# Where the moving operand starts: rows of x shifted by 40 bytes in a one-layer hybrid decoder kernel

## The chip, the cores and the metric

The kernel runs on one core of one Trainium2 chip. The metric is the device time of one execution in microseconds; three runs of the kernel before gave 1689.64, 1690.13 and 1691.94, with the median 1690.13. One further execution was taken with the hardware profiler; all rows of the profile come from that one.

## The reference

One inference step of a decoder layer with three groups of heads, on 256 prompt rows and 8 single-row samples, so 264 rows of 4096 numbers, all in float32. The layer normalises h, projects it with one large matrix, runs three mixers on slices of the projection, gates them, and projects back:

```python
hn = rmsnorm(h, norm_gain)
P = einsum('btd,de->bte', hn, w_in)          # 4096 -> 13324 columns
A = sink_attention(...) * silu(z_a)          # sliding window, 12 heads
B = mlstm_chunkwise(...) * sigmoid(o) * silu(z_m)
C = u * (tril(W_s) @ layernorm(gelu(v)) + b) * silu(z_c)
h = h + concat(A, B, C) @ w_out              # 4096 -> 4096
y = rmsnorm(h, final_gain)
```

Beside y it returns the window's rows of keys and values, the states of B and the normalised rows of C. The two projections hold nearly all of the arithmetic.

## The kernel before, in words

All activations are kept transposed: a row of x in this text is one k-tile of 128 channels, on the 128 partitions, with the 264 positions along the free dimension. There are 32 such rows (KT).

**The projections.** float32 operands are split into a high and a low part of the type float32r, which TensorE streams in one pass. x becomes `xh` and `xl`, a weight tile becomes `wh` and `wl`, and a product is made of three matmuls: wh with xh, wh with xl, wl with xh. The weights are the stationary operand (128 by 128) and a row of xh or xl is the moving one (128 by 264). The output columns are handled in groups of 512: 26 groups for the first matrix and 8 for the second. Each group runs over 16 chunks of two k-tiles; a chunk has four column tiles with two k-tiles each and three matmuls for each, 24 in all, which accumulate into four PSUM tiles named `mp`. That makes 34 x 16 x 24 = 13056 main matmuls.

**The supply of weights.** `load_w` fetches a chunk (512 KB) into one of three `wf` buffers through SyncE's DMA queue, four chunks ahead. `split_w`, two chunks ahead, has ScalarE copy it to `wh` (rounded to the high part) and VectorE subtract to get `wl`. Both have three buffers.

**The rows of x.** `split_x` (lines 244 to 253) writes xh and xl during the first group from `yb`, which holds x; `split_y` (lines 292 to 294) writes them again ahead of the second matrix from the mixers' results, which by then stand in `yb`. Nothing else writes these two tiles, and nothing but the main matmuls and the subtraction that makes xl reads them.

**The order of the work.** Instructions are emitted in one order, written out by hand: ahead of each column tile the small generators of the mixers get a turn (`tick`), when a simple running estimate of each engine's time says that they will not hold up the rest. The estimate goes by the kind of an instruction and the sizes of its operands. So small matmuls of the mixers and transposes stand between main matmuls, on the same engine.

**Places in SBUF.** Bytes are counted within a partition. `xh` starts at 1280 and `xl` at 42240, each with 32 rows of ROW = 320 numbers, 1280 bytes, of which the first 264 numbers are used. Both starts and the row length are multiples of 256. The tile `pad0` ahead of them (PAD0, 32 numbers) makes it so. `yb` follows at 83200 with rows of 264 numbers, 1056 bytes, without padding. A second unused tile, `pad1` (PAD1, 24 numbers), stands ahead of `acc`; the weights come behind that, with `wh` at 136448, 140544 and 144640 and `wl` at 148736, 152832 and 156928. These too are multiples of 256, and a stationary operand starts at a multiple of 512 bytes within its buffer.

The matmuls at the heart of it:

```python
PE.matmul(out, wh[:, kk, s], xh[:, k], start=(k == 0), stop=False)
PE.matmul(out, wh[:, kk, s], xl[:, k], start=False, stop=False)
PE.matmul(out, wl[:, kk, s], xh[:, k], start=False, stop=(k == KT - 1))
```

Line 205 of the profile is the helper through which all engines' calls go, so that groups are told apart by the names of their tiles.

Of the kernel before, what the change touches and what calls it, by code (L numbers as in the profile page):

```python
# [11 lines left out]
F32R = mybir.dt.float32r  # L12
# [6 lines left out]
P = 128  # L19
D = 4096  # L20
KT = D // P
TP = 256
TS = 8
T = TP + TS
# [45 lines left out]
LAG = 6.0  # L70
NCH = KT // KK
ROW = 320
PAD0, PAD1 = 32, 24

SM = {}
# [15 lines left out]
def body(tc, xt, wi, wg, wo, sm, kc, vc, c0, wst, w00, bs, cgain, cbias,  # L91
# [3 lines left out]
    with ExitStack() as ctx:  # L95
        cp = ctx.enter_context(tc.tile_pool(name="const", bufs=1))
# [28 lines left out]
        keep = Phase("keep")  # L125

        cp.tile([P, PAD0], F32, name="pad0")
        xh = cp.tile([P, KT, ROW], F32R, name="xh")[:, :, :T]
        xl = cp.tile([P, KT, ROW], F32R, name="xl")[:, :, :T]
        yb = cp.tile([P, KT, T], F32, name="yb")  # L130
        sms = cp.tile([P, NSM], F32, name="sms")
        ones = cp.tile([P, P], F32, name="ones")
# [1047 lines left out]
```

## Time and profile before

| | |
|---|---|
| median of three runs | 1690.13 us |
| the profiled execution | 1690.53 us |
| its span, first to last instruction | 1687.7 us |
| TensorE busy | 1663.3 us, 13754 matmuls |
| VectorE busy | 911.6 us |
| ScalarE busy | 739.1 us |
| DMA, mean | 195 GB/s |
| mean granted TensorE clock | 0.995 |

Times in a profile are microseconds unless marked ns. PE is TensorE's matmuls, PEld its weight loads, DVE VectorE, ACT ScalarE, POOL GpSimd, SPq SyncE's queue. A row of a group has the output and the inputs by their names in the program, the shapes, the count, the busy time with the mean of one instruction, and then the idle time of the engine just ahead of these instructions with what ended it. In a list of one tile's instructions the three numbers are the shortest, the median and the longest in ns. In a table of windows a row has the stretch, its length, the busy time with the count of records that overlap the stretch, the granted clock, the DMA engines' mean share and GB/s. In a timeline a row has the start in us from the start of the span, the duration, the engine and the instruction; in the chain of waits, the start, the time and the count. Matmuls are pipelined: a record of one lasts longer than the time to the next one's start.

### The profile page before, as it was taken

The numbers are of one execution on the slowest core, as the hardware profiler recorded it, in microseconds if no ns is written. First come the engines' busy times: TensorE is split into PE (matmuls) and PEld (weight loads), VectorE is DVE, ScalarE is ACT, GpSimd is POOL, SyncE is SP. The second block draws the span as 40 slices with busy tenths as digits, with TensorE's granted clock in tenths as the row PEclk, the third lists the DMA queues.
The fourth block names the chain that finished last, engine by engine and source line by source line (L and its number), as shares of the span: only waits on it lengthen the run. The fifth ranks groups of instructions, "written<-read, shape, count | busy, mean of one in ns | idle before, by whom it ended". The sixth has DMA issues, their size and how long they took to land.

```text
span 1687.7 us, 32534 instructions
## 1 busy us (share of the span) xinstructions
PE 1663.3 (99%) x13754; PEld 1646.4 (98%) x13754; DVE 911.6 (54%) x1277; ACT 739.1 (44%) x971; POOL 80.9 (5%) x82
## 2 busy tenths in 40 slices
PE   9999999999999999999999999999999999999995
PEld 9999999999999999999999999999999999999995
DVE  6565644555544455556665666444666554444445
ACT  6554433444434343444444444334454444344442
POOL 0000000000000000001001100000100030000002
PEclk9999999999999999999999999999999999999998
DMA  8555568545455555667767666555656656555553
GB/s 297 172 181 178 184 191 278 157 156 165 151 173 178 184 179 184 205 205 234 229 215 241 216 226 214 185 179 185 204 176 224 203 192 192 187 180 184 180 182 147
DMA packets 102177, 328.91 MB, mean 195 GB/s; under 512 B 11090, under 2 KB 24328, under 8 KB 102032
## 3 DMA queue, kind: packets, MB, share of 16 engines
q1 hardware_dynamic: 101072, 326.04, 60.4%
q8 instruction: 107, 1.75, 0.4%
q10 hardware_dynamic: 960, 0.81, 0.1%
q14 instruction: 38, 0.31, 0.0%
HBM read 314.20 MB, written 12.60 MB: 194 GB/s over the span
## 4 chain that ended last, share of the span: by engine, by line
PE 96%; DVE 2%; DMA 1%; ACT 1%; issue 0%; SPq 0%; DVEq 0%; ACTq 0%
PE mp L205 92%; PE mx L205 3%; DVE wl L205 1%; DVE yb L205 1%; DMA wf<-wo 1%; PE sn L205 0%; ACT wh L205 0%; DMA wf<-wi 0%; PE gps L205 0%; DVE rstd L205 0%; DVE TM L205 0%; ACT es L205 0%; DVE mvs L205 0%; ACT L205 0%; ACT yb L205 0%
## 5 line engine op out<-in xcount | busy, mean ns | idle before, releaser
L205 PE MATMUL mp<-xh,wh 128*128 128x264 f32 x4352 | 1242.5, 286 | 2.5 <-ACT wh L205 1.9
L205 PE MATMUL mp<-xh,wl 128*128 128x264 f32 x4352 | 1231.3, 283 | 2.6 <-DVE wl L205 2.5
L205 PE MATMUL mp<-xl,wh 128*128 128x264 f32 x4352 | 1230.9, 283 | 0.0
L205 DVE TENSOR_TENSOR wl<-wf,wh 128x1024 fp32r<-128x1024 f32 (+1 forms) x545 | 685.3, 1261 | 741.1 <-ACT wh L205 734.5
L205 ACT ACTIVATE wh<-wf 128x1024 fp32r<-128x1024 f32 (+1 forms) x545 | 574.9, 1057 | 808.6 <-PE mp L205 712.1
L205 PEld LDWEIGHTS mp<-xh,wh 128*128 128x128 f32 x4352 | 819.0, 188 | 9.3 <-issue 5.6
L205 PEld LDWEIGHTS mp<-xh,wl 128*128 128x128 f32 x4352 | 819.0, 188 | 3.9 <-DVE wl L205 3.9
L205 PEld LDWEIGHTS mp<-xl,wh 128*128 128x128 f32 x4352 | 819.2, 188 | 0.4
L205 POOL TENSOR_TENSOR acc<-acc,es 128x264 f32<-128x264 f32 x29 | 21.9, 756 | 412.4 <-ACT es L205 410.3
L205 ACT ACT_TABLE_LOAD x22 | 28.2, 1283 | 1.2 <-PEq L1160 0.8
L205 POOL TENSOR_SCALAR_AFFINE_SELECT tmp<-bc 128x128 f32<-128x128 f32 x12 | 5.1, 448 | 491.8 <-DMA bc<-gd 446.0
L205 ACT ACTIVATE es<-yb 128x264 f32<-128x264 f32 x37 | 15.2, 412 | 17.7 <-DVE yb L205 17.7
L205 POOL TENSOR_TENSOR cb<-cb,bc 128x2056 f32<-128x2056 f32 x6 | 22.5, 3748 | 0.2 <-PE mx L205 0.2
L205 ACT ACTIVATE bias<-bias,ar 128x128 f32<-128x128 f32 (+1 forms) x24 | 10.7, 448 | 24.9 <-DVE ar L205 24.8
L205 POOL MEMSET pad<- 128x1024 f32 x2 | 1.9, 950 | 409.5 <-PE mx L205 409.5
L205 ACT ACTIVATE es<-et 128x264 f32<-128x264 f32 x32 | 12.6, 419 | 17.1 <-DVE yb L205 13.8
L205 DVE SCALAR_TENSOR_TENSOR cb<-vb,wsk,cb 128x257 f32<-128x257 f32 x48 | 20.1, 481 | 0.0
L205 ACT ACTIVATE xh<-yb 128x264 fp32r<-128x264 f32 x32 | 12.1, 412 | 17.7 <-DVE yb L205 17.7
L205 DVE TENSOR_TENSOR et<-mp,rstd 128x264 f32<-128x264 f32 x52 | 18.8, 424 | 0.0
L205 ACT ACTIVATE yb<-yb,sms 128x264 f32<-128x264 f32 x32 | 16.5, 517 | 1.0
L205 DVE TENSOR_TENSOR yb<-yb,rstd 128x264 f32<-128x264 f32 x32 | 16.1, 559 | 0.0
L205 DVE TENSOR_TENSOR xl<-yb,xh 128x264 fp32r<-128x264 f32 x32 | 12.7, 429 | 3.9 <-ACT xh L205 3.9
(177 smaller groups left out, 467.4 us busy)
## 6 DMA issues: line engine op xcount, KB each, us to landing
wf<-wi SPq DMA_DIRECT2D x415, 512.0 KB, 3.4
wf<-wo SPq DMA_DIRECT2D x128, 512.0 KB, 3.4
cb<-c SPq DMA_DIRECT2D x12, 514.0 KB
o_cs<-cb SPq DMA_DIRECT2D x12, 514.0 KB, 6.3
vb<-vsd SPq DMA_DIRECT2D x12, 512.0 KB, 4.6
yb<-xt SPq DMA_DIRECT2D x34, 132.0 KB, 3.4
yb<-xt SPq DMA_DIRECT2D x15, 264.0 KB, 7.3
o_y<-yb SPq DMA_DIRECT2D x7, 528.0 KB, 3.2
```

The source lines that it names most:

```text
L205: return fn(*a, **k)
```

## The change

A new constant XOFF = 10. The slices of `xh` and `xl` that all of the kernel uses begin ten numbers, 40 bytes, into each row of 320 instead of at its beginning. The tiles, the rows and everything else in SBUF stay where they are; ten of the 56 unused numbers of a row now stand ahead of the used ones and 46 behind.

```diff
 ROW = 320
+XOFF = 10
 PAD0, PAD1 = 32, 24
...
         cp.tile([P, PAD0], F32, name="pad0")
-        xh = cp.tile([P, KT, ROW], F32R, name="xh")[:, :, :T]
-        xl = cp.tile([P, KT, ROW], F32R, name="xl")[:, :, :T]
+        xh = cp.tile([P, KT, ROW], F32R, name="xh")[:, :, XOFF:XOFF + T]
+        xl = cp.tile([P, KT, ROW], F32R, name="xl")[:, :, XOFF:XOFF + T]
         yb = cp.tile([P, KT, T], F32, name="yb")
```

## The prediction

> **What bounds the kernel now.** I read the page from the top: busy shares, then the chain of work that ended last, then the costliest groups.
>
> ```profile
> span 1687.7 us, 32534 instructions
> PE 1663.3 (99%) x13754; PEld 1646.4 (98%) x13754; DVE 911.6 (54%) x1277; ACT 739.1 (44%) x971; POOL 80.9 (5%) x82
> ...
> PE mp L205 92%; PE mx L205 3%; DVE wl L205 1%; DVE yb L205 1%; DMA wf<-wo 1%; PE sn L205 0%; ACT wh L205 0%; DMA wf<-wi 0%; PE gps L205 0%; DVE rstd L205 0%; DVE TM L205 0%; ACT es L205 0%; DVE mvs L205 0%; ACT L205 0%; ACT yb L205 0%
> ...
> L205 PE MATMUL mp<-xh,wh 128*128 128x264 f32 x4352 | 1242.5, 286 | 2.5 <-ACT wh L205 1.9
> L205 PE MATMUL mp<-xh,wl 128*128 128x264 f32 x4352 | 1231.3, 283 | 2.6 <-DVE wl L205 2.5
> L205 PE MATMUL mp<-xl,wh 128*128 128x264 f32 x4352 | 1230.9, 283 | 0.0
> L205 DVE TENSOR_TENSOR wl<-wf,wh 128x1024 fp32r<-128x1024 f32 (+1 forms) x545 | 685.3, 1261 | 741.1 <-ACT wh L205 734.5
> L205 ACT ACTIVATE wh<-wf 128x1024 fp32r<-128x1024 f32 (+1 forms) x545 | 574.9, 1057 | 808.6 <-PE mp L205 712.1
> ```
>
> The reader is to see one thing: 3 x 4352 = 13056 main matmuls are 92% of the chain, and TensorE hardly waits ahead of them (2.5, 2.6 and 0.0 us). The weight split is far from deciding: ScalarE stands 712.1 us waiting for matmuls to free a buffer of the high parts. So the time is 13056 times the step from the start of one main matmul to the start of the next, plus some 110 us that the change doesn't touch (1690.5 less 13056 x 0.121 us). The 283 ns of a record are not that step, since matmuls overlap; I read the step in the timeline, first in a quiet stretch.
>
> ```profile
> 709.78 0.28 PE L205 MATMUL mp<-xh,wl 128*128 128x264 f32 x1
> 709.90 0.28 PE L205 MATMUL mp<-xh,wh 128*128 128x264 f32 x1
> ...
> 710.74 0.28 PE L205 MATMUL mp<-xl,wh 128*128 128x264 f32 x1
> ```
>
> Eight steps take 0.96 us: 120.0 ns each. Elsewhere the steps are uneven, in two manners:
>
> ```profile
> 614.94 0.28 PE L205 MATMUL mp<-xh,wh 128*128 128x264 f32 x1
> 615.05 0.28 PE L205 MATMUL mp<-xl,wh 128*128 128x264 f32 x1
> 615.18 0.28 PE L205 MATMUL mp<-xh,wl 128*128 128x264 f32 x1
> 615.30 0.28 PE L205 MATMUL mp<-xh,wh 128*128 128x264 f32 x1
> 615.42 0.28 PE L205 MATMUL mp<-xl,wh 128*128 128x264 f32 x1
> ```
>
> Here four steps take 0.48 us, again 120 each on average, but one of them is short (0.11) and one long (0.13). In the other manner five steps make a round:
>
> ```profile
> 519.99 0.29 PE L205 MATMUL mp<-xh,wh 128*128 128x264 f32 x1
> 520.00 0.19 PEld L205 LDWEIGHTS mp<-xl,wh 128*128 128x128 f32 x1
> 520.12 0.28 PE L205 MATMUL mp<-xl,wh 128*128 128x264 f32 x1
> ...
> 520.60 0.29 PE L205 MATMUL mp<-xh,wl 128*128 128x264 f32 x1
> ```
>
> Five steps take 0.61 us, 122 ns each. The windows over single column groups show how often. A window counts every record that overlaps it, so about 2.3 (0.28 over 0.12) more than start in it.
>
> ```profile
> 507.00:552.00 45.00, 45.00 (x373) 1.00 0.59 182
> 600.50:645.50 45.00, 45.00 (x377) 1.00 0.59 186
> 693.00:738.00 45.00, 45.00 (x378) 1.00 0.66 210
> 1045.50:1090.50 45.00, 45.00 (x371) 1.00 0.58 181
> 1523.50:1568.50 45.00, 45.00 (x372) 1.00 0.58 181
> 62.00:105.00 43.00, 43.00 (x361) 1.00 0.57 176
> ```
>
> 377 and 378 in 45 us are 120.0 ns; 371 to 373 are 121.4 to 122.0 (45 us over 373 - 2.3 and over 371 - 2.3). Of twelve such windows after 500 us eight are of the slow manner and four of the fast one, with the clock at 1.00 in all; the second group (361 in 43 us) and its neighbours are fast. With the same instructions in each group, what chooses the manner is not in the program.
>
> **The change, part by part.** (1) Instructions: none is added, removed or reordered. The slices keep their 264 columns, the rows their 1280 bytes, the pool its size, so every other tile, the weights among them, stays at its address; the order planner works from sizes, which are the same. No wait, no DMA, no semaphore is moved. All of it is in how long existing instructions take.
>
> (2) The writers of xh and xl: 32 + 32 rows twice, 128 instructions on ScalarE and VectorE. No row of the profile writes a row 40 bytes off, but the rows of yb are 1056 bytes apart and so lie at eight different places behind a multiple of 256, and the groups that write them hardly spread:
>
> ```profile
> L205 DVE TENSOR_TENSOR yb<-mp,yb x32: 423/423/433, 1334.1 to 1663.0; 128x264 f32<-128x264 f32 x32
> L205 ACT ACTIVATE yb<-mp x8: 373/392/394, 57.3 to 106.7; 128x264 f32<-128x264 f32 x8
> ```
>
> From the spreads (10 and 21 ns), a bound of 21 ns either way each, 128 x 0.021 = 2.7 us of engine time. It lies under the matmuls, whose cover is ScalarE's 712.1 us of waiting; without that cover it would be at most 2.7 us. I take nothing.
>
> (3) The moving read of the 13056 main matmuls, the whole question. The floor of a step comes from the four-byte matmuls, which stream at half the pace:
>
> ```profile
> 315.03 0.81 PE L205 MATMUL mx<-pt,vtok 128*128 128x256 f32 x4
> 315.68 0.49 PE L205 MATMUL mx<-sms,bias 128*128 128x128 f32 x3
> ```
>
> These four are two of 256 and two of 128 columns; the next group starts 0.65 us later, so 0.65 / 768 = 0.846 ns for a column. At twice that pace 264 columns would take 264 x 0.423 = 112 ns, an estimate. The main step is 120.0 to 121.4, so 8 to 9 ns of each are not streaming. They vary with no regard to the operand (the groups of all three kinds have 283 to 286 ns). They come in fixed rounds, and a weight load starts within 10 ns of each matmul (520.00 after 519.99). The one thing that recurs with each matmul, and could cost a varying piece of it, is the weight read running beside the moving read. Today both begin on a multiple of 256, so they meet at the same relation each time; the change moves one by ten columns against the other, 10 x 0.423 = 4.2 ns of streaming. That is as long as the swing between 0.11 and 0.12, so it can move the rounds. No row has this relation in it, so the step is bounded from both sides: 112 (nothing left but streaming) below, 126 above (the longest steps, 0.13 in the row at 615.05, rounded). Between them I take the one that is already a steady state of this hardware in this kernel, the even 120.0: the nearest row, and one that needs only that the slow round no longer catches.
>
> The sum: the first three groups (1152 matmuls) run at 120.0 already. For the rest I use two long rows of the chain:
>
> ```profile
> 1051.27 186.36 PE mp L205 x1542
> 1361.41 302.41 PE mp L205 x2498
> ```
>
> At 120.0 ns these 4040 would take 484.8 us instead of 488.8; the last matmul's tail (0.16 us beyond its step) in each leaves 3.6 us, 0.9 ns for one; with the fast windows of the middle, 0.85. So 11904 x 0.85 = 10.1 us. The profiled execution took 1690.53 us (span 1687.7 and 2.8 around it), 0.4 above the median of the runs, 1690.13. 1690.1 - 10.1 = **1680 us**. With TensorE faster by 0.6%, next in line would be the split at 1.06 + 1.26 us per 24 steps of 0.12 (2.88 us), which has 0.5 us left even one after the other.
>
> [...]
>
> **The rivals.**
>
> *The two reads come apart altogether* (faster by much more). For: the 8 to 9 ns above the estimate of streaming need a cause, and rounds with steps of 0.11 show that single matmuls do better than 120. Against: in none of the windows does a stretch stay below 120.0. If all steps were as the short ones, 116 (0.11 to 0.12, as the starts are rounded), 13056 x (120.8 - 116) = 63 us: **1627**; at 112 it would be 115 us: 1575. The split would then have 24 x 0.116 = 2.78 us per chunk against 2.32, still enough; the loads go with TensorE's pace and stand at a DMA share of 0.59 in the windows.
>
> [...]
>
> *The new relation is worse* (slower). The place is the same, the start of the moving read, which would find the weight read in its way more often or begin within a unit of the memory. For: steps of 0.13 exist, so losing 10 ns in one matmul is possible; nothing makes 40 bytes better than 0 by itself. [...] A step of 126 always would cost 13056 x 5.2 = 68 us: 1758. Point: a step of 123.5, the middle of 121 and 126, 13056 x 2.7 = 35 us: **1725**. It decides from the point where the mean step passes 121.4, that of the slow round today. Against: even the slow round costs 1.4 ns only.
>
> *The address does not matter* (no change): **1690**. The rounds would then come from the engine's own queue, not from the memory. For: the three groups of main matmuls, which read different rows and weights, agree within 3 ns. Against: the round changes from group to group with the same instructions, so it hangs on something as fine as a phase, and ten columns are 4.2 ns of phase. That the change does not do what it says is excluded by the addresses.
>
> [...]
>
> **How the numbers follow.** Forecast 0.30 (own range 1676 to 1686), much faster 0.22, no change 0.20, slower 0.28. Faster by over 0.2%: 0.30 + 0.22 = 0.52; within 0.2% (3.4 us, about what a measurement of this kernel tells from no change) 0.20; slower 0.28. The range of 8 in 10: below, the much faster case to its point, 1627, leaving out about half of it (0.11); above, the slower case a little past its point, to 1730, leaving out a third (0.09). So 1627 to 1730.
>
> **What would show it.** The mean step: count in windows of 45 us inside the groups. 377 or 378 everywhere is the forecast; 385 or more the much faster rival; 371 or fewer the slower one; the same mix of 371 to 374 and 377 the last. Rounds of four or five that differ from today's would show that the relation counts, even at an equal time. Writers of the rows as long as now would confirm part 2 (the medians 502, 489, 410 and 428 ns below); waits of matmuls for wh, wl or wf grown above today's few us would show the split as the next bound. Wrong it is if main steps change in groups of one kind only, or if the time moves with the steps unchanged.
>
> ```profile
> L205 DVE SCALAR_TENSOR_TENSOR xl<-yb,sms,xh x32: 484/489/494, 3.6 to 46.7; 128x264 fp32r<-128x264 f32 x32
> L205 ACT ACTIVATE xh<-yb x32: 404/410/427, 1234.9 to 1329.2; 128x264 fp32r<-128x264 f32 x32
> L205 DVE TENSOR_TENSOR xl<-yb,xh x32: 426/428/435, 1236.2 to 1329.7; 128x264 fp32r<-128x264 f32 x32
> L205 ACT ACTIVATE xh<-yb,sms x30: 497/502/514, 8.0 to 45.4; 128x264 fp32r<-128x264 f32 x30
> ```

## The result, and the profile after

The changed kernel takes 1721.21 us (median of four runs, 1720.00 to 1721.67) where the kernel before took 1689.89 in the same comparison: a ratio of 1.0182, 95% interval 1.0164 to 1.0199. It is **slower** by 31 us, 1.8%. The forecast was 1680; the time lies inside the stated range of 1627 to 1730, at the slower rival's end of it.

The page of the kernel after: the span and the busy times, and the groups that answer to those shown of before.

```profile
span 1719.9 us, 32534 instructions
PE 1697.6 (99%) x13754; PEld 1681.1 (98%) x13754; DVE 909.0 (53%) x1277; ACT 739.1 (43%) x971; POOL 80.4 (5%) x82
...
L206 PE MATMUL mp<-xh,wh 128*128 128x264 f32 x4352 | 1252.7, 288 | 1.6 <-ACT wh L206 1.1
L206 PE MATMUL mp<-xh,wl 128*128 128x264 f32 x4352 | 1243.6, 286 | 1.4 <-DVE wl L206 1.3
L206 PE MATMUL mp<-xl,wh 128*128 128x264 f32 x4352 | 1242.9, 286 | 0.0
L206 DVE TENSOR_TENSOR wl<-wf,wh 128x1024 fp32r<-128x1024 f32 (+1 forms) x545 | 685.7, 1261 | 775.5 <-ACT wh L206 769.3
L206 ACT ACTIVATE wh<-wf 128x1024 fp32r<-128x1024 f32 (+1 forms) x545 | 574.8, 1057 | 842.2 <-PE mp L206 765.1
```

The instructions are the same, 32534, and the split costs what it did (1261 and 1057 ns). ScalarE's wait for matmuls has grown from 712 to 765 us: TensorE is the late one. All three groups of main matmuls have grown alike, by 2 to 3 ns a record. The windows, over the same stretches as of before where the prediction shows them:

```profile
62.00:105.00 43.00, 43.00 (x349) 1.00 0.55 172
507.00:552.00 45.00, 45.00 (x365) 1.00 0.57 176
600.50:645.50 45.00, 45.00 (x365) 1.00 0.56 177
693.00:738.00 45.00, 45.00 (x365) 1.00 0.61 201
1092.50:1137.50 45.00, 45.00 (x369) 1.00 0.59 179
1523.50:1568.50 45.00, 45.00 (x365) 1.00 0.57 178
```

365 in 45 us is a step of 45 / (365 - 2.3) = 124.1 ns, where before it was 120.0 or 121.4, at the same granted clock of 1.00. The window at 1092 us begins in a group of the third quarter that runs at 120 still, so the even round has not disappeared; it has become rare. Some 14% of the steps lie in stretches of twelve that take about 1440 ns, against some 45% before. The timeline shows the new round:

```profile
719.83 0.29 PE L206 MATMUL mp<-xh,wl 128*128 128x264 f32 x1
719.95 0.28 PE L206 MATMUL mp<-xh,wh 128*128 128x264 f32 x1
720.07 0.29 PE L206 MATMUL mp<-xl,wh 128*128 128x264 f32 x1
720.20 0.29 PE L206 MATMUL mp<-xh,wl 128*128 128x264 f32 x1
720.32 0.28 PE L206 MATMUL mp<-xh,wh 128*128 128x264 f32 x1
720.45 0.29 PE L206 MATMUL mp<-xl,wh 128*128 128x264 f32 x1
```

Five steps take 0.62 us, 124 each: no short step of 0.11 is left. Below, **the mean step** of a kernel is the mean of all steps in its trace from one main matmul to the next one that follows directly, those above 140 ns (stops) left out: some 12820 of the 13056. It was 120.75 ns before and is 123.43 after. 13056 x 2.68 = 35 us, and the stops, counted beyond 120 ns each, add up to 2.6 us less now (20.9 and 18.3 us); that leaves 32.4, beside the 32.2 by which the profiled span grew (1687.7 to 1719.9). So the whole of the slowdown is the step. Each mean step comes from one profiled execution, and single executions of one kernel differ by a few us, so that differences of a few tenths of a nanosecond between kernels are read from the ratios instead.

The writers of the rows, which part (2) of the prediction costed at nothing, in the lists of the two tiles:

```profile
L206 DVE SCALAR_TENSOR_TENSOR xl<-yb,sms,xh x32: 486/491/495, 3.6 to 46.1; 128x264 fp32r<-128x264 f32 x32
L206 DVE TENSOR_TENSOR xl<-yb,xh x32: 426/429/435, 1257.7 to 1352.9; 128x264 fp32r<-128x264 f32 x32
```

```profile
L206 ACT ACTIVATE xh<-yb x32: 405/410/427, 1256.4 to 1352.4; 128x264 fp32r<-128x264 f32 x32
L206 ACT ACTIVATE xh<-yb,sms x30: 499/502/516, 7.5 to 44.8; 128x264 fp32r<-128x264 f32 x30
```

The medians are 491, 429, 410 and 502 ns, against 489, 428, 410 and 502: ScalarE's and VectorE's writes differ by at most 2 ns.

### The profile page after: what moved, and what is told of

It reads as the page before. It is cut to its first block, busy times and chain, and to the rows that moved or that the text cites. A ratio compares the mean times of both kernels' runs of the same rounds, so it can differ in the third digit from the quotient of the medians.

```text
span 1719.9 us, 32534 instructions
## 1 busy us (share of the span) xinstructions
PE 1697.6 (99%) x13754; PEld 1681.1 (98%) x13754; DVE 909.0 (53%) x1277; ACT 739.1 (43%) x971; POOL 80.4 (5%) x82
## 4 chain that ended last, share of the span: by engine, by line
PE 96%; DVE 1%; DMA 1%; ACT 0%; issue 0%; SPq 0%; DVEq 0%; ACTq 0%
PE mp L206 93%; PE mx L206 3%; DVE yb L206 1%; DMA wf<-wo 1%; DMA wf<-wi 0%; DVE wl L206 0%; PE sn L206 0%; ACT wh L206 0%; PE gps L206 0%; DVE rstd L206 0%; DVE TM L206 0%; DVE mvs L206 0%; ACT L206 0%; DVE es L206 0%; SPq L979 0%
## 5 line engine op out<-in xcount | busy, mean ns | idle before, releaser
L206 DVE TENSOR_TENSOR wl<-wf,wh 128x1024 fp32r<-128x1024 f32 (+1 forms) x545 | 685.7, 1261 | 775.5 <-ACT wh L206 769.3
L206 ACT ACTIVATE wh<-wf 128x1024 fp32r<-128x1024 f32 (+1 forms) x545 | 574.8, 1057 | 842.2 <-PE mp L206 765.1
```

The source lines that it names most:

```text
L206: return fn(*a, **k)
```

## The experiments

All edits below are to the changed kernel, except that of `n272`, which is to the kernel before. The labels give the bytes by which the x rows (x) and the weights (w) lie behind a multiple of 256. Ratios are to the kernel before, with 95% intervals; it was run again beside each set and took 1688.0 to 1691.9 us there, so ratios and steps compare two experiments better than their times do.

### Is it the distance between the two reads?

The theory on record was that the moving read and the weight read, both starting on a multiple of 256, get in each other's way. Its test is to shift the weights as well. That takes another layout of the split weights, whose three buffers become one tile with room ahead; a control has that layout with nothing shifted.

```diff
+        wha = wp.tile([P, 3 * 1024 + 64], F32R, name="wh", bufs=1)
+        wla = wp.tile([P, 3 * 1024 + 64], F32R, name="wl", bufs=1)
+        def weight(a, n):
+            o = WOFF + 1024 * (n % 3)
+            return a[:, o:o + 1024].rearrange("p (k n) -> p k n", k=KK)
...
-            hi = wp.tile([P, KK, 512], F32R, name="wh")
-            lo = wp.tile([P, KK, 512], F32R, name="wl")
+            hi = weight(wha, n)
+            lo = weight(wla, n)
```

The control, XOFF = 0 and WOFF = 0:

> Control: x rows at a multiple of 256 as before, the three buffers of wh and of wl in one tile each (and so at other addresses, all still multiples of 256). Both theories: the steps of before, rounds of 120.0 and 121.3 ns, and 1687 to 1693 us. If it differs by more than 5 us, other runs with this layout are read against it and not against the kernel before.

Measured: 1691.84 us, ratio 0.9998 (0.9989 to 1.0007), mean step 120.82 ns. The layout is neutral with the rows at 0.

Both shifted, XOFF = 10 and WOFF = 10:

> x rows and the stationary weights both 40 bytes behind a multiple of 256. Theory R (the relation of the moving read to the weight read sets the step): the relation is that of before, so steps of 120.0 and 121.3 ns and 1690 us (1685 to 1695). Theory A (the place of the row itself, whatever the weights): rounds of 124.0 ns as in the changed kernel and 1721 us (1715 to 1727).

Measured: 1720.35 us, ratio 1.0167 (1.0152 to 1.0182), mean step 123.37 ns. Two of its windows:

```profile
507.00:552.00 45.00, 45.00 (x367) 1.00 0.61 177
1523.50:1568.50 45.00, 45.00 (x367) 1.00 0.60 176
```

With the distance of before restored, it is as slow as with the rows alone shifted (367 against 365). The theory of the distance falls, as the account of this slowdown.

Only the weights shifted, XOFF = 0 and WOFF = 10:

> x rows on multiples of 256, only the weights 40 bytes behind. R: the relation is neither that of before nor that of the changed kernel (it is its mirror), so the mean step leaves 120.7 ns, by some 1 to 5 ns either way (1675 to 1755 us, not 1687 to 1693). A: 120.0 and 121.3 ns, 1690 us.

Measured: 1695.95 us, ratio 1.0025 (1.0016 to 1.0035), mean step 121.32 ns, in one round of five in all groups. A small effect of 4 us, an eighth of the change's. The time lies inside R's wide range, but the step moved by only 0.5 ns from the control's, less than the 1 to 5 of R, and A had no effect at all. It isn't nothing, so the weights' place counts a little.

### What about the place of a row?

One number is changed in each of these:

```diff
-XOFF = 10
+XOFF = 8        # x32; 2: x8, 4: x16, 12: x48, 16: x64, 6: x24, 1: x4, 20: x80, 26: x104
```

> x rows 32 bytes behind a multiple of 256, two whole pieces of 16 bytes instead of two and a half. A with pieces of 16 or 32 bytes: as before, 1690 us. A with pieces of 64 bytes (264 columns at 32 bytes end on a multiple of 64, 17 pieces as before): 1690 us. R: another mean step than 120.7 or 123.4 ns is possible, 112 to 126; 1690 us would speak against R with a unit above 32 bytes.

Measured: 1706.26 us, ratio 1.0083 (1.0067 to 1.0100), mean step 122.16. About half of the slowdown is there at 32 bytes already, so whole pieces of 16 or 32 bytes are not all there is to it.

> x rows 8 bytes behind a multiple of 256. Theory P (a row is fetched in pieces of 64 bytes; 8 + 1056 bytes lie in 17 pieces, as at 0 and at 32): mean step 120 to 122.3 ns, 1687 to 1710 us. Theory L (pieces of 16 bytes; the row begins within one, as at 40, and touches 67 instead of 66): slow as at 40, 123.4 to 124 ns, 1715 to 1725 us. Theory D (the later the start within 64 bytes, the longer): a little over 0's, 121 to 122 ns, 1691 to 1700 us.

Measured: 1714.25 us, ratio 1.0144 (1.0127 to 1.0161), mean step 122.80. Eight bytes are worse than 32. L comes nearest, a little high; P and D missed.

> x rows 16 bytes behind. P: 17 pieces of 64 bytes, 120 to 122.3 ns, 1687 to 1710 us. L: whole pieces of 16 bytes, as at 0, 1687 to 1693 us. D: between 0 (120.8 ns) and 32 (122.2 ns), 1693 to 1703 us.

Measured: **1681.23 us**, ratio 0.9950 (0.9935 to 0.9964), mean step 120.01: faster than the kernel before, and than the times of all three theories. L and P, both from 1687, miss it by the same 6 us; the step lies at the lower end of P's range.

> x rows 48 bytes behind, a multiple of 16. P: 48 + 1056 bytes lie in 18 pieces of 64, as at 40, 123.4 to 124.5 ns, 1715 to 1728 us. L: whole pieces of 16 bytes as at 0, 1687 to 1693 us. D: longer than at 40, over 124 ns, over 1722 us.

Measured: 1698.63 us, ratio 1.0054 (1.0039 to 1.0069), mean step 121.47. This is 6 us above L's range and 16 below P's. P and D, by which it should have been at least as slow as 40, are out; L has missed as well.

> x rows 64 bytes behind. P, L and D: as at 0, rounds of 120.0 and 121.3 ns, 1687 to 1693 us. A unit above 64 bytes (128 or 256): another mean step, 121 to 126 ns, over 1695 us.

Measured: 1690.41 us, ratio 1.0003 (0.9994 to 1.0012), mean step 120.75. The time is that at 0, but the rounds are not (122, 120 and 118 ns in the second group, no round of five later), so two places with one mean can differ in their rounds.

> x rows 24 bytes behind: 8 more than a multiple of 16. If beginning within a piece of 16 bytes costs time by itself (8 was slower than 0 and 16, 40 slower than 32 and 48): 122 to 123.5 ns a step, 1706 to 1723 us, slower than both 16 (1681) and 32 (1706). If only the place within 64 bytes counts: between the two, 120.0 to 122.2 ns, 1681 to 1706 us.

Measured: 1708.44 us, ratio 1.0118 (1.0103 to 1.0133), mean step 122.29. It is slower than its neighbours 16 and 32, as the first half of the expectation has it, though hardly slower than 32 (122.16).

> x rows 4 bytes behind a multiple of 256. If any start within 16 bytes costs: 122 to 124 ns, 1705 to 1725 us, as at 8 (1714). If it takes a start in the second half of 16 bytes: 120 to 121.3 ns, 1681 to 1693 us.

Measured: 1741.84 us, ratio 1.0297 (1.0278 to 1.0317), mean step 124.67: the slowest of all places, slower than either line said. The rows of x4's three groups of main matmuls, and then windows of x4, x8 and x16 in this order:

```profile
L206 PE MATMUL mp<-xh,wh 128*128 128x264 f32 x4352 | 1266.3, 291 | 1.1 <-ACT wh L206 0.6 <-DVE et L206 0.5
L206 PE MATMUL mp<-xh,wl 128*128 128x264 f32 x4352 | 1257.7, 289 | 1.7 <-DVE wl L206 1.5
L206 PE MATMUL mp<-xl,wh 128*128 128x264 f32 x4352 | 1255.6, 289 | 0.0
```

```profile
1523.50:1568.50 45.00, 45.00 (x358) 1.00 0.59 175
1600.00:1645.00 45.00, 45.00 (x358) 1.00 0.59 175
```

```profile
1523.50:1568.50 45.00, 45.00 (x369) 1.00 0.60 177
1600.00:1645.00 45.00, 45.00 (x367) 1.00 0.62 188
```

```profile
1523.50:1568.50 45.00, 45.00 (x376) 1.00 0.60 182
1600.00:1645.00 45.00, 45.00 (x377) 1.00 0.57 175
```

358, 367 to 369 and 376 to 377 in 45 us, with the clock at 1.00 and matmuls hardly waiting for a weight: the order 4, 8, 16 is in the step itself. At 4 bytes the same stretch of 45 us holds 18 to 19 matmuls fewer than at 16. The profiled execution of x4 took 1736.23 us, 5.6 under the median, so its usual step is longer still by some 0.4 ns, an estimate (5.6 us over 13056 steps).

> x rows 80 bytes behind, 64 + 16. If the place counts modulo 64 (or less): as at 16, every pair of steps 240 ns, 1678 to 1684 us. If more than 64 counts: something else, over 1686 us.

Measured: 1694.66 us, ratio 1.0029 (1.0017 to 1.0042), mean step 121.17. It is not as 16 (ratio 0.9950), so the place counts beyond 64 bytes.

> x rows 104 bytes behind, 64 + 40. If the place counts modulo 64: as at 40, 123.4 ns, 1715 to 1725 us. If more than 64 counts, but beginning within 16 bytes costs as well: 122 ns or more, over 1704 us. If neither: 1681 to 1700 us.

Measured: 1721.94 us, ratio 1.0185 (1.0170 to 1.0200), mean step 123.39: as at 40. This agrees with either of the first two lines of its expectation; x80 rules the first out as a general rule.

Put together, with the weights on multiples of 256:

| x rows behind a multiple of 256 by | mean step, ns | median, us |
|---|---|---|
| 0 (before) | 120.75 | 1689.89 |
| 16 | 120.01 | 1681.23 |
| 32 | 122.16 | 1706.26 |
| 48 | 121.47 | 1698.63 |
| 64 | 120.75 | 1690.41 |
| 80 | 121.17 | 1694.66 |
| 8 | 122.80 | 1714.25 |
| 24 | 122.29 | 1708.44 |
| 40 (after) | 123.43 | 1721.21 |
| 104 | 123.39 | 1721.94 |
| 4 | 124.67 | 1741.84 |

The six multiples of 16 have a mean of 121.05 ns (120.01 to 122.16), the four places 8 bytes behind such a multiple 122.98 (122.29 to 123.43): 1.9 ns more, and 4 bytes is worse still. The closest pair, 24 and 32, differs by no more than 0.13 ns, but the intervals of its ratios are apart. Against the mean of its two neighbours 8 is 2.4 slower, 24 is 1.2 and 40 is 1.6. The multiples of 16 differ by up to 2.1 ns among themselves, by something that the place within 64 bytes does not settle (16 against 80). A row is 66 x 16 bytes long, so a row that begins off a multiple of 16 also ends off one: whether the beginning or the end costs was not tested.

### One part of the rows alone

```diff
-        xl = cp.tile([P, KT, ROW], F32R, name="xl")[:, :, XOFF:XOFF + T]
+        xl = cp.tile([P, KT, ROW], F32R, name="xl")[:, :, :T]
```

> xh rows 40 bytes behind, xl rows on multiples of 256: two of three main matmuls read a shifted row. If each row's own place sets its step: (2 x 123.4 + 120.75) / 3 = 122.5 ns, 1711 to 1716 us. If the cost comes from the relation of a row to the one read before it: more than with all rows shifted alike, over 123.4 ns, over 1721 us.

Measured: 1717.41 us, ratio 1.0170 (1.0155 to 1.0185), mean step 123.17. That is above the sum by rows (122.5) and not above the whole change. By the kind of the matmul, the steps that begin with wh and xh have a mean of 125.7, those with xl 121.1, and those with wl and xh 122.8; the second xh reader costs much less than the first. Nothing simple adds up here: what a step costs hangs on more than its own row's place.

### The number of columns

Both kernels have XOFF = 0, the rows of before.

> x rows as before, but the wh by xl and the wl by xh matmuls stream 256 columns instead of 264, except for the last k-tile: this leaves the correction terms of the eight sample positions out. By columns alone (0.42 ns each): 8 x 0.42 x 2/3 = 2.2 ns less, 118.5 ns, 1661 us. If a row goes in pieces of 16 columns (64 bytes), 16 instead of 17: 6.7 x 2/3 = 4.4 ns less, 116.3 ns, 1633 us.

```diff
-                    PE.matmul(out, wh[:, kk, s], xl[:, k], start=False, stop=False)
-                    PE.matmul(out, wl[:, kk, s], xh[:, k], start=False, stop=(k == KT - 1))
+                    m = T if k == KT - 1 else TP
+                    PE.matmul(out[:, :m], wh[:, kk, s], xl[:, k, :m], start=False, stop=False)
+                    PE.matmul(out[:, :m], wl[:, kk, s], xh[:, k, :m], start=False, stop=(k == KT - 1))
```

Measured: 1667.68 us, ratio 0.9875 (0.9860 to 0.9889), mean step 119.02. 1.7 ns less, nearer to the 2.2 estimated for columns alone than to 4.4.

> x rows as before, but all main matmuls stream 272 columns, 264 of the row and 8 zeros behind it, that nothing reads afterwards; the zeros are written once. By columns alone: 3.4 ns more, 124.1 ns, 1734 us. If a row goes in pieces of 64 bytes, 17 either way: 120.0 to 121.3 ns, 1690 us.

```diff
+        xhw, xlw = xhw[:, :, :T + 8], xlw[:, :, :T + 8]
...
-                    PE.matmul(out, wh[:, kk, s], xh[:, k], start=(k == 0), stop=False)
+                    PE.matmul(wide, wh[:, kk, s], xhw[:, k], start=(k == 0), stop=False)
```

The other two matmuls of the three are changed in the same way.

Measured: 1746.82 us, ratio 1.0344 (1.0327 to 1.0361), mean step 125.45: 4.7 ns more, over the 3.4 estimated for columns alone, as n256 was under its 2.2. Fetching in pieces of 64 bytes, where this step would have been free, is out.

### Does the start of the weights cost by itself?

```diff
-XOFF = 10
+XOFF = 4        # x16_w8, x16_w16; 0: x0_w8
+WOFF = 2        # x16_w8, x0_w8; 4: x16_w16
```

All three have the layout of the control, one tile each for wh and wl.

> x rows 16 bytes behind, the stationary weights 8 bytes behind a multiple of 256 (the buffers of wh and of wl in one tile each). If only the moving operand's place counts: 120.0 ns, 1678 to 1685 us. If a stationary start within 16 bytes costs as much: 121.5 to 123 ns, 1700 to 1720 us.

Measured: 1704.20 us, ratio 1.0081 (1.0066 to 1.0096), mean step 121.91, 1.9 ns over x16. This looked like the second line of the expectation.

> x rows on multiples of 256, the weights 8 bytes behind. If a stationary start within 16 bytes costs by itself, as x16_w8 suggests (1.9 ns): 122.6 ns, 1710 to 1717 us. If the distance between the two counts instead (8 bytes one way in x8, the other way here): 121 to 123 ns. If neither: as the control, 1687 to 1694 us; the weights at 40 gave 1696.

Measured: 1680.87 us, ratio 0.9958 (0.9941 to 0.9974), mean step 120.04. This lies outside all three lines. The weights' start within 16 bytes costs nothing here; against the control (120.82) it even gains. So the second line of x16_w8's expectation falls. The windows of x16_w8 and then of x0_w8:

```profile
1523.50:1568.50 45.00, 45.00 (x371) 1.00 0.59 180
1600.00:1645.00 45.00, 45.00 (x371) 1.00 0.59 178
```

```profile
1523.50:1568.50 45.00, 45.00 (x377) 1.00 0.58 185
1600.00:1645.00 45.00, 45.00 (x377) 1.00 0.57 176
```

371 and 377 with the weights at the same place. With the weights on multiples of 256 rows at 16 are faster than rows at 0 (120.01 and 120.75 ns); with the weights at 8 they are slower (121.91 and 120.04). So beside the rows' own place there is a pairing of the two after all, worth up to 1.9 ns.

> Both operands 16 bytes behind a multiple of 256. If only the start within 16 bytes of either operand counts, and the row's place for the rest: 120.0 ns as with the rows alone at 16, 1678 to 1685 us. If the distance of the two counts: as with both at 0, rounds of 120.0 and 121.3 ns, 1687 to 1694 us.

Measured: 1681.32 us, ratio 0.9957 (0.9942 to 0.9972), mean step 120.06, the even round nearly everywhere. As with the rows alone at 16, though the distance is that of before.

**The fastest** are x16, x0_w8 and x16_w16, all about 0.5% faster than the kernel before and at 120.0 ns; they can't be told apart. x16 is the least change: XOFF = 4 instead of 10.

## Why the prediction was wrong

**What bounds** held: 13056 steps set the time, and nothing else moved it by more than the 2.6 us of the stops. **Part (1)**, no instruction changed, and **part (2)**, the writers, held.

**Part (3)** failed, at the value chosen between the bounds: the even round at 120.0 ns, on the ground that the slow round would no longer catch. Instead of 0.85 ns gained on each step of the sum, the step lost 2.68, from 120.75 to 123.43. The bounds, 112 and 126, held it. The reason behind the choice was that the weight read beside the moving read is the one thing that recurs with each matmul and could cost a varying piece, so that moving away from equal places could free it. x40_w40 took that reason away: with equal places again at 40 bytes, the step is 123.37, and x16_w16, with equal places too, has 120.06. The moving read recurs as well, and what counts first is where its row lies: off a multiple of 16 bytes, 1.9 ns more on the mean of the places tried. That the place of the row sets the slowdown is shown; by what mechanism it does is not.

The trace of before had no row that could show this, since all rows of xh and xl began on a multiple of 256. The spread of the writers' rows was evidence on other engines only. The floor of 112 ns rests on the main matmuls streaming at exactly twice the pace of a record of the four-byte ones. That factor was the author's estimate. In the trace of before a main matmul is one record (13056 of both) and a four-byte one that is no transpose is two (`mx<-pt,vtok`: 12 calls with 256 columns, 24 records); such records of 264 columns (`mx<-acc,ones`, `mx<-et,ones`) start 222 ns apart (two in 0.45 us from 1664.11), 1.84 times the main step of 120.75 and 1.93 times the shortest one of 115. Eight columns fewer or more moved the step by amounts on both sides of the estimated pace (n256 1.7 ns for 2.2, n272 4.7 for 3.4).

**The slower rival** was right in sign and size. Of its two mechanisms the weight read in the way falls with x40_w40, and a start within a unit of the memory would fit the places 8 bytes off, 1.9 ns slower on the mean. With a unit of 16 bytes the runs agree for the moving operand (x8, x24 and x40 are 2.4, 1.2 and 1.6 ns over their neighbours), and with x0_w8 not for the stationary one (120.04 ns, the control 120.82). But the count of pieces of 16 that a row touches, 67 off a multiple and 66 on one, is not shown to be the cause: rows at 4, 8, 24, 40 and 104 all touch 67, at 122.29 to 124.67 ns, and at 4 the step is 1.9 ns longer than at 8. The rival's point, 123.5 ns and 1725 us, is close to the 123.43 and 1721 measured by luck, for it was the middle of two bounds and no working from a mechanism. By the table, 1.6 of the 2.68 ns at 40 stand above its neighbours 32 and 48, and these two stand 1.1 above 0 for a reason that stays open. Its chance, 0.28, was too small beside 0.30: a start that is aligned more coarsely is the one thing that the change took away, and nothing in the profile made 40 bytes better than 0, as the prediction itself said.

**Much faster** is refuted for all places tried: with 264 columns no kernel's mean step came below 120.0, though the kernel before has 384 single steps of 115. **No change** is refuted: 123.43 ns against 120.75. The place of the weights matters too: x16_w8 and x16_w16, with the same rows and layout, have 121.91 and 120.06 ns. Whether the two reads meet there is not shown.

**What stays open**: by what mechanism a start off 16 bytes costs time, and why 4 costs more than 8; why 32 and 48 are slower than 0, 16 and 64; what the pairing with the weights' place is; and what makes the rounds. The place of the accumulators and the order of the three matmuls were not varied.

## What to carry to other kernels

In this kernel, where TensorE streams float32r rows and hardly waits (5.1 us ahead of the main matmuls before), the start of the moving operand is a knob of the order of 1 to 3% (ratios from 0.9950 at 16 bytes to 1.0297 at 4). Where another kernel is like it, try rows that begin on a multiple of 16 bytes, and a few such multiples, for the best (16) and the worst (32) of them differ by 1.5% here. Read it in the count of matmuls in equal windows, not in the records' durations, and move nothing else while doing so. When a change takes an alignment away and no row of the trace shows a price for that, the slower side deserves the larger chance: of the ten places tried beside 0, eight were slower, one the same (64) and one faster (16).

## What was not expected of the hardware

The steps settle into rounds that repeat for whole groups, and the rounds' sums are the same within a nanosecond wherever they occur: 480 ns for four steps and 606 or 607 for five before, 620 for five after, 240 for two in x16 (124 and 116 in turn), 366 or 367 for three in x32 (118, 124 and 125). Three quite different placements come to 120.01, 120.04 and 120.06 on the mean and none goes below.

A step depends on more than its own row: with only xh shifted, the two readers of xh had 125.7 and 122.8 ns, with different weights and different neighbours. And eight more columns cost 4.7 ns a step where the streaming estimate was 3.4, so what a step takes beyond that estimate (some 8 ns before) is no constant either.
